# Ordering the experts by their token counts on the chip, with loads addressed from registers and a switch between programs of two and three slot groups

## The chip, the core and the metric

The kernel runs on one core of one Trainium2 chip. The metric is the device time of one execution in microseconds. The engines are TensorE (PE, with PEld for its weight loads), VectorE (DVE), ScalarE (ACT), GpSimd (POOL) and SyncE (SP); SP computes nothing here and issues the weight loads. Each engine has a sequencer that runs its own list of instructions in order.

## What is computed

The reference is a trunk of two layers over 256 tokens of 1024 channels. Each layer mixes tokens (windowed attention beside an mLSTM) and then channels. The channel step of the first layer is a dense SwiGLU; that of the second layer, which the change touches, picks two of eight experts for each token:

```python
def swiglu(x, w13, w2):
    a, g = jnp.split(x @ w13, 2, axis=-1)
    return (jax.nn.silu(a) * g) @ w2

def moe_ffn(x, router_w, router_b, w13, w2):
    logits = (x @ router_w).astype(jnp.float32) + router_b.astype(jnp.float32)
    top_v, top_i = lax.top_k(logits, TOP_K)          # TOP_K = 2 of N_EXPERTS = 8
    wts = jax.nn.softmax(top_v, axis=-1)
    gate = jnp.einsum('bsk,bske->bse', wts, jax.nn.one_hot(top_i, N_EXPERTS, ...))
    y = jnp.zeros_like(x)
    for e in range(N_EXPERTS):
        y = y + gate[..., e:e + 1] * swiglu(x, w13[e], w2[e])
    return y
```

An expert's `w13` is 1024 x 7168 and its `w2` 3584 x 1024, all float32, 44 MB an expert. How many tokens an expert gets is known only when the router has run; the mean is 64.

## The kernel before

Up to the router the kernel runs two mixers and the dense layer; the change leaves that part as it is. `route_tile` picks the experts, writes `posm` (for each token and expert its place among the expert's tokens, or -1), `gate`, and `cnti`, the largest count.

The experts run one after the other (`one_pass`, loop over `e`). Each has 96 slots (`CAP`) in three groups (`NG`) of 32 (`G`). `one_hot` compares `posm` with a ramp, and `gather` multiplies the tokens with it, which gives the expert's tokens transposed (`xe`); this is done for a batch of experts at once (experts 0 and 1, 2 to 4, 5 to 7). The weights are the moving operand of PE and come in pieces of 1 MB, 42 an expert: 28 of `w13` (in four rounds of columns, `ROUNDS`) and 14 of `w2`. For each piece the loop in `batch` issues the products of all three groups; a group has its own 32 columns of the array's weights, and the four quarters of PE's columns work on four column blocks side by side, so that a piece's matmuls go by the number of groups. After a round ACT and DVE apply the SwiGLU; `turn` transposes the hidden rows on PE; `turned_hot` and `scatter` bring the results back to their tokens, and DVE adds them to `x` with the gate. These smaller jobs are put into a list (`todo`) and run behind the second or third piece of a later round.

The pieces are loaded by `Stream`: one list in the order of use, 14 places of 1 MB in the expert stage (`RING`), one DMA each on SP's queue (`pump`, line 89). A piece's load is issued when `done` frees its place, which is when PE has used the piece 14 further up. Which expert a load takes its bytes from is written into the program.

Behind the pass every engine loads `cnti` into a register (line 1034) and jumps twice over a second and third pass (line 1036), which would run for tokens past 96 and 192; with these inputs neither runs (336 loads are 8 x 42). Then the last normalisation and the output follow.

The framework orders the instructions of each engine by a list scheduler; within a pool tile with one buffer the next user waits for the last one.

Of the kernel before, what the change touches and what calls it, by code (L numbers as in the profile page):

```python
# [17 lines left out]
P = 128  # L18
S = 256
# [28 lines left out]
ROUNDS = ((0, 512, (3, 0, 1, 2)), (2048, 512, (0, 1, 2, 3)), (4096, 512, (0, 1, 2, 3)), (6144, 256, (0, 1, 2, 3)))  # L48
RING = ("ring",) * 4 + ("part",) * 6 + ("XL", "XH") + ("more",) * 2


class Stream:
# [3 lines left out]
    def __init__(self, tc, part_pool, part_bufs):  # L56
        self.tc, self.nc, self.behind = tc, tc.nc, None
        self.part_pool, self.part_bufs = part_pool, part_bufs
        self.pieces, self.parts = [], []
        self.raw, self.ready = {}, {}  # L60
        self.places, self.used = {}, {}
        self.loaded = self.split = self.taken = 0
        self.whole_i = -1

# [10 lines left out]
    def pump(self):  # L75

        while self.loaded < len(self.pieces):
# [8 lines left out]
            t = pool.tile([P, n], F32, name="w_raw", tag=tag, bufs=bufs)  # L86
# [43 lines left out]
    def get(self):  # L130
        return self.take(1)[0]

# [10 lines left out]
def hybrid_trunk_kernel(ctx: ExitStack, tc: tile.TileContext, *aps):  # L143
# [71 lines left out]
    def add_experts(s):  # L215


        count = 0

        def to_ring(src):  # L220
            nonlocal count
            s.add(src, (), RING[count % len(RING)])
            count += 1

        for e in range(E):
            w13, w2 = a["exp_w13"][0, e], a["exp_w2"][0, e]
            for c0, w, order in ROUNDS:
                n = 2048 // (4 * w)
                for r0 in range(0, D, n * P):
                    to_ring(w13[r0:r0 + n * P, c0:c0 + 4 * w].rearrange("(k p) f -> p k f", p=P))  # L230

            for r0 in (*range(512, 2048, 256), 0, 256, *range(2048, D_FE, 256)):
                to_ring(rview(w2, r0, 256))

    add_experts(st)
# [17 lines left out]
    rw = const.tile([P, KD, E], F32, name="rw")  # L253
    relb = biasp.tile([NB, HA], F32, name="relb")
# [160 lines left out]
    def router_weights():  # L415
# [4 lines left out]
        nc.vector.memset(ones_b, 1.0)  # L420

# [6 lines left out]
    def route_tile(tt, xt):  # L428
# [24 lines left out]
        if tt:  # L453
            cnt = small.tile([P, 1], F32, name="cnt", tag="cnt")
# [371 lines left out]
    def experts(l, xt):  # L826
# [7 lines left out]
        for t in sides:  # L834
            nc.vector.memset(t[:, NG - 1], 0.0)
# [5 lines left out]
        def aux(shape, name):  # L841
            return pe.tile(shape, F32, name=name, tag="aux", bufs=2)
# [13 lines left out]
        BATCHES = {0: (2, P), 2: (3, CAP), 5: (3, CAP)}  # L856

        def one_pass(s, base):
            pm = posm
            if base:  # L860
                pm = ep.tile([P, 2, E], F32, name="posb")
                nc.vector.tensor_scalar(pm, posm, float(-base), None, op0=ALU.add)
            hot = {}

            def one_hot(e):

                n, w = BATCHES[e]
                t = e2.tile([P, 2, n, w], F32R, name="oneh", tag="oneh")
                for tt in range(2):
                    nc.vector.tensor_tensor(t[:, tt], iota[:, 0:w].unsqueeze(1).to_broadcast([P, n, w]),  # L870
                                            pm[:, tt, e:e + n].unsqueeze(2).to_broadcast([P, n, w]), op=ALU.is_equal)
                hot[e] = t

            def gather(e):

                n, w = BATCHES[e]
                t = e2.tile([P, KD, n, w], F32, name="xe", tag="xe")
                for k in range(KD):
                    pt = aux([P, n, w], "xe")
# [11 lines left out]
            def turned_hot(e):  # L891

                o = e2.tile([P, 2, NG, 4, G], F32, name="hot4", tag="hot4", bufs=1)
# [4 lines left out]
                t = e2.tile([P, NG, S], F32, name="oneT", tag="oneT", bufs=1)  # L898
                for g0, n in ((0, 2), (2, 1)):
                    pt = aux([P, 2, S], "oT")  # L900
# [7 lines left out]
            def scatter(e, i, y, oneT):  # L908

                big, one = side(i).rearrange("p a (t b) -> p a t b", t=2), aux([P, 2, 256], "sc1")  # L910
                for tt in range(2):
                    for g in range(NG):
                        for b in range(4):
# [3 lines left out]
                                             stop=(g == NG - 1), skip_group_check=True)  # L917
                for tt in range(2):
                    for b in range(4):
                        o = big[:, b, tt] if b < NG else one[:, tt]  # L920
                        xt_ = x[:, tt, b * 256:(b + 1) * 256]
                        nc.vector.scalar_tensor_tensor(xt_, o, gate[:, tt, e:e + 1], xt_, op0=ALU.mult, op1=ALU.add)

            def turn(hT, ht, slot, n):

                for g in range(NG):
                    pt = aux([P, n, 4, G], "hT")
# [5 lines left out]
            def turn_one(hT, h4):  # L933

                pt = aux([P, 4, CAP], "hT")
                for i in range(4):
                    nc.tensor.transpose(pt[:, i], h4[:, i * P:(i + 1) * P], ident[0:CAP, 0:CAP])
                nc.vector.tensor_copy(hT[:, 16:20, :], pt)

            with tc.high_priority():  # L940
                one_hot(0)
            xe = gather(0)
            if not base:
                nc.scalar.activation(x, x, AF.Copy, scale=ALPHA)
            todo = []

            def run_todo():
                for f in todo:
                    f()
                todo.clear()  # L950

            def batch(e, n, products, at):

                for k in range(n):
                    i, piece = s.whole()
                    for g in range(NG):
                        products(g, k, piece)
                    s.done(i)
                    if k == at:
                        run_todo()  # L960
            n_side = 0
            for e in range(E):
                if e in BATCHES:
                    cur, first_e = xe, e
                hT = e2.tile([P, D_FE // P, CAP], F32, name="hT", tag="hT", bufs=1)
                hA = e2.tile([P, NG, 512], F32, name="hA", tag="hA", bufs=1)
                hC = e2.tile([P, NG, 256], F32, name="hC", tag="hC", bufs=1)
                s4 = e2.tile([P, NG, 512], F32, name="s4", tag="s4", bufs=1)
                h4 = s4[0:CAP, 0]
                for r, (c0, w, order) in enumerate(ROUNDS):  # L970
                    pt = side(n_side)
                    n_side += 1
                    ks = 2048 // (4 * w)

                    def products(g, n, piece):
                        for j in range(ks):
                            k = n * ks + j
                            for c in range(4):
                                o = order.index(c)
                                mm = nc.tensor.matmul(pt[c * G:(c + 1) * G, g, 0:w],  # L980
                                                      cur[:, k, e - first_e, g * G:(g + 1) * G],
                                                      piece[:, j, o * w:(o + 1) * w], start=(k == 0),
                                                      stop=(k == KD - 1), skip_group_check=True)
                        return mm.ins

                    batch(e, KD // ks, products, 2 if ks == 1 else 1)
                    q = [slice(c * G, (c + 1) * G) for c in range(4)]
                    if r == 0:
                        for g in range(NG):
                            nc.scalar.activation(hA[:, g], pt[:, g], AF.Silu)  # L990
                    elif r == 1:
                        nc.vector.tensor_mul(hA[q[3]], hA[q[3]], pt[q[3]])  # L992
                        nc.scalar.activation(s4[q[3]], pt[q[0]], AF.Silu)  # L993
                        for c in range(4):
                            src = pt[q[1 + c // 2], :, (c % 2) * 256:(c % 2) * 256 + 256]
                            nc.scalar.activation(hC[q[c]], src, AF.Silu)
                    elif r == 2:
                        for g in range(NG):
                            nc.vector.tensor_mul(hA[0:CAP, g], hA[0:CAP, g], pt[0:CAP, g])  # L999
                        for g in range(NG):  # L1000
                            nc.vector.tensor_mul(h4[q[g]], s4[q[3], g], pt[q[3], g])
                        todo.append(lambda hT=hT, hA=hA, h4=h4: (turn(hT, hA, 0, 4), turn_one(hT, h4)))
                    else:
                        nc.vector.tensor_mul(hC, hC, pt[:, :, 0:256])
                        todo.append(lambda hT=hT, hC=hC: turn(hT, hC, 20, 2))
                if e + 1 in BATCHES:
                    one_hot(e + 1)
                    xe = gather(e + 1)
                oneT = turned_hot(e)
                acc = side(n_side)  # L1010
                nf = D_FE // P
                for f0 in range(0, nf, nf // 2):
                    def products(g, n, piece):
                        for j in range(2):
                            f = f0 + 2 * n + j
                            for b in range(4):
                                mm = nc.tensor.matmul(acc[b * G:(b + 1) * G, g, 0:256], hT[:, f, g * G:(g + 1) * G],  # L1017
                                                      piece[:, j, b * 256:(b + 1) * 256], start=(f == 0),
                                                      stop=(f == nf - 1), skip_group_check=True)
                        return mm.ins  # L1020

                    batch(e, nf // 4, products, 2)
                y = e2.tile([P, NG, 256], F32, name="y", tag="y", bufs=1)
                for g in range(NG):
# [4 lines left out]
                todo.append(lambda e=e, i=n_side, y=y, oneT=oneT: scatter(e, i, y, oneT))  # L1029
                n_side += 1  # L1030
            run_todo()

        one_pass(st, 0)
        over = nc.values_load(cnti[0:1, 0:1], min_val=0, max_val=S)
        for base in range(CAP, S, CAP):
            with tc.If(over > base):
# [6 lines left out]
                add_experts(s2)  # L1043
# [66 lines left out]
```

## Time and profile before

| | us |
|---|---|
| median of 3 runs (lowest, highest) | 1582.56 (1582.51, 1584.98) |
| the profiled execution | 1585.02 |
| its span in the profile | 1583.2 |
| mean granted TensorE clock in it | 0.989 |
| PE busy / DVE / ACT | 1544.6 / 508.0 / 378.4 |
| bytes read from HBM | 452.04 MB |

In the profile, PE is the matmuls and PEld the loads of their stationary operand, which run beside them. A float32 matmul is recorded as two. A "q" behind an engine's name is its sequencer. The rows of a window give busy time and count of each engine, then the granted TensorE clock (1.00 is 2.4 GHz, 0.50 is 1.2 GHz), the mean busy share of the 16 DMA engines, and GB/s. The share can pass 1, as it adds the times of packets that overlap.

### The profile page before, as it was taken

The page shows a single profiled execution, that of the slowest core. Times are in us where ns is not written, and L with a number is a line of the kernel's source. Part 1 is how long each engine was busy: PE and PEld are TensorE (multiplying, and loading weights), DVE is VectorE, ACT ScalarE, POOL GpSimd, SP SyncE. Part 2 cuts the span into 40 slices and gives each one's busy share as a digit, 9 for nine tenths or more (in the row PEclk, how much of TensorE's full clock was granted, in tenths as well). Part 3 has the DMA queues.
Part 4 walks back from the last instruction along what each step waited for, and adds up shares of the span by engine and source line. Part 5 has one row for each costly group of instructions (what it writes and reads, how often), then busy time and mean ns, then how long its engine had stood idle before and what let it go on. Part 6 is the DMA issues. An engine that isn't in the chain of part 4 may idle for free. (4 is left out here: it accounts for less than half of the span.)

```text
span 1583.2 us, 35559 instructions
## 1 busy us (share of the span) xinstructions
PE 1544.6 (98%) x16296; PEld 959.3 (61%) x16296; DVE 508.0 (32%) x970; ACT 378.4 (24%) x540; POOL 31.0 (2%) x44
## 2 busy tenths in 40 slices
PE   7999999999999999999999999999999999999994
PEld 6889989998888984354354354354355354354353
DVE  5577775544857763010020010010020010010012
ACT  4555444443445522100110100100110100100100
POOL 2000000000100000000000000000000000000000
PEclk9999999999999997999999999999999999999997
DMA  9634555555533578999979999999979999999950
GB/s 319 194 134 147 179 184 185 186 185 186 181 126 115 166 263 318 390 373 378 392 285 377 390 374 378 390 373 378 391 291 372 390 373 378 399 365 378 387 207 30
DMA packets 112004, 455.55 MB, mean 288 GB/s; under 512 B 7456, under 2 KB 9744, under 8 KB 87264
## 3 DMA queue, kind: packets, MB, share of 16 engines
q1 hardware_dynamic: 108608, 443.05, 74.8%
q0 software_dynamic: 2944, 9.49, 2.1%
q8 instruction: 131, 2.15, 0.5%
q10 hardware_dynamic: 288, 0.59, 0.1%
q14 instruction: 33, 0.27, 0.1%
HBM read 452.04 MB, written 2.63 MB: 287 GB/s over the span
## 5 line engine op out<-in xcount | busy, mean ns | idle before, releaser
L980 PE MATMUL side<-w_raw,xe 128*32 128x512 f32 (+1 forms) x6144 | 592.3, 541 | 0.0
L980 PEld LDWEIGHTS side<-w_raw,xe 128*32 128x32 f32 x6144 | 199.0, 110 | 378.2 <-issue 346.8
L1017 PE MATMUL side<-w_raw,hT 128*32 128x256 f32 x5376 | 302.0, 380 | 0.0
L105 DVE TENSOR_TENSOR w_part<-w_raw,w_part 128x1024 fp32r<-128x1024 f32 x170 | 206.1, 1221 | 141.7 <-ACT w_part L103 141.4
L1017 PEld LDWEIGHTS side<-w_raw,hT 128*32 128x32 f32 x5376 | 173.1, 110 | 116.9 <-issue 6.3
L313 PE MATMUL mm<-xh,w_part 128*128 128x256 f32 x832 | 238.4, 287 | 0.0
L311 PE MATMUL mm<-xh,w_part 128*128 128x256 f32 x832 | 237.7, 286 | 0.0
L312 PE MATMUL mm<-xl,w_part 128*128 128x256 f32 x832 | 237.2, 286 | 0.0
L103 ACT ACTIVATE w_part<-w_raw 128x1024 fp32r<-128x1024 f32 x170 | 179.0, 1058 | 218.3 <-PE mm L313 185.1
L313 PEld LDWEIGHTS mm<-xh,w_part 128*128 128x128 f32 x832 | 159.0, 191 | 4.5 <-issue 4.3
L311 PEld LDWEIGHTS mm<-xh,w_part 128*128 128x128 f32 x832 | 159.1, 191 | 4.2 <-issue 3.8
L312 PEld LDWEIGHTS mm<-xl,w_part 128*128 128x128 f32 x832 | 159.1, 191 | 3.5 <-issue 3.3
L1026 DVE COPY y<-side 128x256 f32<-128x256 f32 x8 | 3.4, 425 | 281.1 <-ACT y L1028 281.1
L992 DVE TENSOR_TENSOR hA<-hA,side 32x1536 f32<-32x1536 f32 x8 | 14.1, 1760 | 247.7 <-issue 247.7
L931 ACT ACTIVATE hT<-hT 128x512 f32<-128x512 f32 (+1 forms) x48 | 21.8, 489 | 238.2 <-PE hT L929 238.2
L999 DVE TENSOR_TENSOR hA<-hA,side 96x512 f32<-96x512 f32 x24 | 15.0, 679 | 150.3 <-PE side L980 150.3
L1028 ACT ACTIVATE y<-side 128x256 f32<-128x256 f32 x16 | 6.1, 383 | 213.2 <-PE side L1017 209.3
L990 ACT ACTIVATE hA<-side 128x512 f32<-128x512 f32 x24 | 12.6, 598 | 169.1 <-PE side L980 169.1
L993 ACT ACTIVATE s<-side 32x1536 f32<-32x1536 f32 x8 | 11.5, 1438 | 166.6 <-DVE hA L992 166.6
L311 PE MATMUL mm<-w_part,xh 128*128 128x512 f32 (+1 forms) x128 | 48.3, 380 | 2.7 <-ACT w_part L103 2.2
L312 PE MATMUL mm<-w_part,xh 128*128 128x512 f32 (+1 forms) x128 | 47.7, 373 | 2.2 <-DVE w_part L105 2.2
L313 PE MATMUL mm<-w_part,xl 128*128 128x512 f32 (+1 forms) x128 | 47.9, 374 | 1.6 <-DVE xl L280 1.6
(275 smaller groups left out, 1272.5 us busy)
## 6 DMA issues: line engine op xcount, KB each, us to landing
w_raw<-in_exp_w_dram SPq DMA_DIRECT2D x336, 1024.0 KB, 6.8
w_raw<-in_ffn_w_dram SPq DMA_DIRECT2D x33, 1024.0 KB, 5.1
w_raw<-in_w_in_dram SPq DMA_DIRECT2D x18, 1024.0 KB, 6.0
w_raw<-in_w_gate_dram SPq DMA_DIRECT2D x16, 1024.0 KB, 5.1
w_raw<-in_w_o_dram SPq DMA_DIRECT2D x8, 1024.0 KB, 4.9
w_raw<-in_w_br_a_dram SPq DMA_DIRECT2D x4, 1024.0 KB, 5.2
w_raw<-in_w_br_m_dram SPq DMA_DIRECT2D x4, 1024.0 KB, 5.1
w_raw<-in_w_in_dram SPq DMA_DIRECT2D x4, 512.0 KB, 8.4
```

The costliest lines, as they stand in the source:

```text
L103: self.nc.scalar.activation(hi, src, AF.Copy)
L105: self.nc.vector.tensor_sub(lo, src, hi.bitcast(F32))
L311: nc.tensor.matmul(ps_ap, lh, rh, start=start, stop=False, **kw)
L312: nc.tensor.matmul(ps_ap, lh, rl, start=False, stop=False, **kw)
L313: nc.tensor.matmul(ps_ap, ll, rh, start=False, stop=stop, **kw)
L931: nc.scalar.activation(dst, pt, AF.Copy)
L980: mm = nc.tensor.matmul(pt[c * G:(c + 1) * G, g, 0:w], cur[:, k, e - first_e, g * G:(g + 1) * G], piece[:, j, o * w:(o + 1) * w], start=(k ...
L990: nc.scalar.activation(hA[:, g], pt[:, g], AF.Silu)
L992: nc.vector.tensor_mul(hA[q[3]], hA[q[3]], pt[q[3]])
L993: nc.scalar.activation(s4[q[3]], pt[q[0]], AF.Silu)
L999: nc.vector.tensor_mul(hA[0:CAP, g], hA[0:CAP, g], pt[0:CAP, g])
L1017: mm = nc.tensor.matmul(acc[b * G:(b + 1) * G, g, 0:256], hT[:, f, g * G:(g + 1) * G], piece[:, j, b * 256:(b + 1) * 256], start=(f == 0), ...
```

## The change

1. `ordering` runs on DVE behind the router. It marks which of experts 1 to 7 have more than 64 tokens and gives the marked ones the places 2, 4, 6, 1, 3, 5, 7 in this order, the others what is left. It writes the expert of each place and the number of the program to `metai`, and copies `posm` and `gate` in the order of the places (`pmP`, `gtP`). Expert 0 stays first. Three small constants are added (`ordc`).
2. SP loads the seven experts from `metai` into registers, and the loads of places 1 to 7 take their address from them.
3. All engines load the number of the program and, behind expert 0, go through one `tc.Switch` with three arms. Arm 0, 1 and 2 hold places 1 to 7 with the first 3, 5 or 7 of the list 2, 4, 6, 1, 3, 5, 7 at three groups and the rest at two. With two groups every loop over groups is shorter: products, SwiGLU, transposes, scatter.
4. The batches of the gather are place 0 (with expert 1's slots beside it, unused), 1 to 3, 4 and 5, 6 and 7: four where there were three.
5. Tiles of the expert stage that came from pools are made once and reused in turn, so that all arms have the same addresses; the memsets of the third bank of `side` go.

```diff
+PLACES = (2, 4, 6, 1, 3, 5, 7)
+ARMS = (3, 5, 7)
...
+            def src():
+                if ordered and e:
+                    i = s.which[e - 1]
+                    return take(w[0, bass.ds(i, 1)].rearrange("a r f -> (a r) f"))
+                return take(w[0, e])
...
-        for t in sides:
-            nc.vector.memset(t[:, NG - 1], 0.0)
...
+        def ordering():
...
+            nc.vector.memset(meta, 0.0)
+            nc.vector.tensor_scalar(big, cnt8[:, 1:E], float(CAP - G), None, op0=ALU.is_gt)
+            nc.vector.tensor_tensor(t49, tri7, across(big), op=ALU.mult)
+            nc.vector.tensor_reduce(pre, t49, X, ALU.add)
+            nc.vector.tensor_reduce(m[:, 0:1], big, X, ALU.add)
...
+            nc.vector.tensor_tensor(sl, place_of.unsqueeze(2).to_broadcast([P, n1, n1]), across(rank), op=ALU.is_equal)
+            for src, dst in ((j7, meta[:, 0:n1]), (posm[:, 0, 1:E], pmP[:, 0, 1:E]), (posm[:, 1, 1:E], pmP[:, 1, 1:E]),
+                             (gate[:, 0, 1:E], gtP[:, 0, 1:E]), (gate[:, 1, 1:E], gtP[:, 1, 1:E])):
+                nc.vector.tensor_tensor(t49, sl, across(src), op=ALU.mult)
+                nc.vector.tensor_reduce(dst, t49, X, ALU.add)
+            nc.vector.tensor_scalar(meta[:, 0:n1], meta[:, 0:n1], 1.0, None, op0=ALU.add)
+            for i, limit in enumerate(ARMS[:-1]):
+                nc.vector.tensor_scalar(meta[:, 9 + i:10 + i], m[:, 0:1], float(limit), None, op0=ALU.is_gt)
...
-                BATCHES = {0: (2, P), 2: (3, CAP), 5: (3, CAP)}
+                BATCHES = {0: (1, P), 1: (3, CAP), 4: (2, P), 6: (2, P)}
...
-                    for g in range(NG):
-                        products(g, k, piece)
-                    s.done(i)
+                        for g in range(ng):
+                            products(g, k, piece)
+                        s.done(i)
...
+            ordering()
+            which.extend(nc.values_load(metai[0:1, i:i + 1], engines=[mybir.EngineType.SP], min_val=1, max_val=E - 1)
+                         for i in range(n1))
+            arm_i = nc.values_load(metai[0:1, 8:9], min_val=0, max_val=len(ARMS) - 1)
+            expert(s, 0, NG, c)
+            for arm in tc.Switch(arm_i, len(ARMS)):
+                sa, ca = s.fork(), dict(c, todo=list(c["todo"]))
+                for e in range(1, E):
+                    expert(sa, e, NG if PLACES.index(e) < ARMS[arm] else NG - 1, ca)
```

On PE, at the passage from expert 0 to the next one, before (a product of a `w2` piece is `side<-w_raw,hT`, one of a `w13` piece `side<-w_raw,xe`, the scatter `<-y,oneT`):

```order
L1017 MATMUL side_5838<-w_raw,hT 32x256 x248
L980 MATMUL side_5839<-w_raw,xe 32x512 x36
L916 MATMUL side_5838<-y,oneT 128x256 x3
L916 MATMUL sc_6849<-y,oneT 128x256
L916 MATMUL side_5838<-y,oneT 128x256 x3
```

And the same place now, in the first arm:

```order
L1111 MATMUL side_5842<-w_raw,hT 32x256 x232
L1136 TENSOR_LOAD metai
L1222 SWITCH_STRIDE
L1222 ISA x2
L1138 BRANCH_PREFETCH_HINT
L1074 MATMUL side_5843<-w_raw,xe_5846 32x512 x24
L1018 MATMUL side_5842<-y,oneT 128x256 x3
```

The switch stands between the last product of expert 0 and the first of the next place, and three pieces are 24 matmuls there where they were 36.

On SP, where the loads of the first 14 expert pieces end, before:

```order
L89 DMA w_raw<-in_exp_w_dram 128x2048 x14
L1034 TENSOR_LOAD cnti
L1034 ISA x2
L89 DMA w_raw<-in_exp_w_dram 128x2048 x10
L89 DMA w_raw<-in_exp_w_dram 128x2x1024 x18
L89 DMA w_raw<-in_exp_w_dram 128x2048 x24
```

And now, to the switch, with six of the eight loads of `metai` and 12 of the 14 loads of place 1 left out between the two fences:

```order
L102 DMA w_raw<-in_exp_w_dram 128x2048 x14
L1146 TENSOR_LOAD cnti
L1146 ISA x2
L1134 TENSOR_LOAD metai
L1134 ISA x2
```

```order
L1136 TENSOR_LOAD metai
L1136 ISA x2
L102 DMA w_raw<-in_exp_w_dram 128x2048 x10
L102 DMA w_raw<-in_exp_w_dram 128x2x1024 x18
L102 ISA
L102 DMA w_raw<-in_exp_w_dram 128x2048
```

```order
L102 DMA w_raw<-in_exp_w_dram 128x2048
L1222 SWITCH_STRIDE
L1222 ISA x2
L1138 BRANCH_PREFETCH_HINT
L102 ISA
```

Behind the 14 loads stand eight register loads more, each load of places 1 to 7 has one instruction in front of it, and SP comes to the switch when 56 loads (42 of expert 0, 14 of place 1) are issued.

On DVE, at the end of the pass, before:

```order
L1026 COPY y<-side_5839 128x256
L922 SCALAR_TENSOR_TENSOR x<-side_5839,gate,x 128x256 x6
L922 SCALAR_TENSOR_TENSOR x<-sc_13284,gate,x 128x256 x2
L1034 TENSOR_LOAD cnti
L1036 COMPARE_AND_BRANCH
```

And now, at the end of the first arm:

```order
L1118 COPY y<-side_5843 128x256
L1024 SCALAR_TENSOR_TENSOR x<-side_5843,gtP,x 128x256 x6
L1024 SCALAR_TENSOR_TENSOR x<-aux_5844,gtP,x 128x256 x2
L1222 UNCONDITIONAL_BRANCH
L1138 BRANCH_PREFETCH_HINT
```

The jump behind the additions leads over the other two arms, to the load of `cnti` and the two branches that stood there before.

## Rows read from the trace of the kernel before

**Rows 1.** The page, parts 1 and 5: engine busy; group | busy us, mean ns | idle before.

```profile
PE 1544.6 (98%) x16296; PEld 959.3 (61%) x16296; DVE 508.0 (32%) x970; ACT 378.4 (24%) x540; POOL 31.0 (2%) x44
...
L980 PE MATMUL side<-w_raw,xe 128*32 128x512 f32 (+1 forms) x6144 | 592.3, 541 | 0.0
...
L1017 PE MATMUL side<-w_raw,hT 128*32 128x256 f32 x5376 | 302.0, 380 | 0.0
```

**Rows 2.** Waits of SP's queue, 640 to 1583 us: total us, times, longest.

```profile
SPq L89 <- PE side L980: 502.5, 214, 5.1
SPq L89 <- PE side L1017: 235.0, 93, 5.9
```

**Rows 3.** Timeline of PE in three stretches: start us, length us, line, tiles, count.

```profile
607.23 5.40 PE L980 MATMUL side<-w_raw,xe 128*32 128x512 f32 x28
...
726.72 7.91 PE L980 MATMUL side<-w_raw,xe 128*32 128x512 f32 x72
...
1532.09 26.97 PE L1017 MATMUL side<-w_raw,hT 128*32 128x256 f32 x496
```

**Rows 4.** Windows of one expert each: length, PE, PEld, DVE, ACT, POOL, clock, share, GB/s.

```profile
971.00:1087.40 116.40, 116.40 (x1520) 51.59 (x1516) 12.09 (x24) 10.58 (x18) 0.00 (x0) 1.00 0.99 383
1087.40:1212.40 125.00, 125.00 (x1552) 56.35 (x1548) 13.91 (x28) 12.33 (x22) 0.00 (x0) 1.00 0.92 352
```

**Rows 5.** Timeline of SP's queue, 721 to 735 us.

```profile
721.78 13.23 SPq L89 DMA_DIRECT2D w_raw<-in_exp_w_dram  x6
```

**Rows 6.** The page, part 6: DMA issues, KB each, median us to landing.

```profile
w_raw<-in_exp_w_dram SPq DMA_DIRECT2D x336, 1024.0 KB, 6.8
```

**Rows 7.** Windows of 40 us in the expert stage.

```profile
800.00:840.00 40.00, 40.00 (x571) 23.21 (x573) 4.54 (x12) 4.26 (x10) 0.00 (x0) 1.00 0.78 285
1360.00:1400.00 40.00, 40.00 (x433) 14.57 (x422) 5.71 (x7) 6.12 (x8) 0.00 (x0) 1.00 1.02 394
```

**Rows 8.** Windows at the highest shares of the DMA engines.

```profile
645.00:650.00 5.00, 5.00 (x52) 1.56 (x48) 0.00 (x0) 0.00 (x0) 0.00 (x0) 1.00 1.04 359
...
600.00:605.00 5.00, 2.82 (x12) 2.10 (x12) 4.57 (x28) 0.55 (x3) 0.00 (x0) 0.50 1.03 428
655.00:685.00 30.00, 30.00 (x336) 11.95 (x328) 5.49 (x8) 6.32 (x8) 0.00 (x0) 1.00 1.02 409
```

**Rows 9.** Timeline of DVE: first of 17 small operations of the router, and the memset behind.

```profile
600.29 0.16 DVE L436 TENSOR_TENSOR route<-lg,rb 128x8 f32<-128x8 f32 x1
...
602.65 0.48 DVE L835 MEMSET side<- 128x512 f32 x1
```

**Rows 10.** Line 1034, the register loads: duration ns min/median/max, first and last start.

```profile
L1034 SPq TENSOR_LOAD <-cnti x1: 461/461/461, 602.6 to 602.6; - x1
...
L1034 SPq FUSED_REGOPS  x1: 182/182/182, 603.1 to 603.1; - x1
...
L1034 PEldq TENSOR_LOAD <-cnti x1: 491/491/491, 1561.9 to 1561.9; - x1
```

**Rows 11.** Line 1036, the two jumps over the second passes, same columns.

```profile
L1036 PEldq COMPARE_BRANCH  x2: 3418/4152/4886, 1562.5 to 1566.1; - x2
L1036 DVEq COMPARE_BRANCH  x2: 56/64/72, 1564.2 to 1567.2; - x2
...
L1036 DVEq EVENT_SEMAPHORE  x2: 21/21/21, 1567.1 to 1571.7; - x2
```

**Rows 12.** Line 89, the loads.

```profile
DMA to landing us min/median/max: 4.7/6.5/13.6
```

**Rows 13.** Timeline of DVE behind the jumps: in brackets idle before and what ended it.

```profile
1571.85 1.29 DVE L298 BATCH_NORM_STATS2 bs<-x 128x6 f32<-128x512 f32 x2 [5.21 <-DVEq L1036]
```

**Rows 14.** Windows with PE partly idle, and the clock behind the second.

```profile
202.40:207.40 5.00, 3.18 (x18) 2.16 (x17) 5.00 (x9) 3.23 (x4) 0.81 (x1) 1.00 0.00 0
588.30:593.30 5.00, 3.06 (x24) 2.73 (x24) 4.93 (x12) 2.14 (x3) 1.20 (x2) 1.00 0.94 328
595.00:600.00 5.00, 4.70 (x24) 4.34 (x23) 4.90 (x19) 4.97 (x6) 0.00 (x0) 0.50 1.00 415
```

More of the change, by code (lines that the diff above doesn't have):

```diff
@@ L1 @@
+import copy
 import math
@@ L131, in get, with fork @@
         return self.take(1)[0]
+    def fork(self):
+        s = copy.copy(self)
+        s.raw, s.used, s.loads = dict(self.raw), dict(self.used), dict(self.loads)
+        return s
 def cols_views(n, w):
@@ L906, in turned_hot, with scatter @@
                 return t
-            def scatter(e, i, y, oneT):
-                big, one = side(i).rearrange("p a (t b) -> p a t b", t=2), aux([P, 2, 256], "sc1")
+            def scatter(e, i, y, oneT, ng):
+                big, one = side(i).rearrange("p a (t b) -> p a t b", t=2), aux([P, 2, 256])
                 for tt in range(2):
-                    for g in range(NG):
+                    for g in range(ng):
                         for b in range(4):
@@ L961, in one_pass @@
-            n_side = 0
-            for e in range(E):
-                if e in BATCHES:
[L964 to L969, printed above, removed]
+                    nc.tensor.transpose(pt[:, i], h4[0:ng * G, i * P:(i + 1) * P],
+                                        ident[0:ng * G, 0:ng * G])
@@ new lines, in turn_one, with expert, run_todo, batch @@
+                nc.vector.tensor_copy(hT[:, 16:20, 0:ng * G], pt)
+            def expert(s, e, ng, c):
+                if e in BATCHES:
+                    c["cur"], c["first"] = c["xe"], e
+                cur, j0 = c["cur"], e - c["first"]
+                def run_todo():
+                    for f in c["todo"]:
+                        f()
+                    c["todo"] = []
+                def batch(n, products, at):
+                    for k in range(n):
+                        i, piece = s.whole()
+                        for g in range(ng):
+                            products(g, k, piece)
+                        s.done(i)
+                        if k == at:
+                            run_todo()
@@ L977, in products @@
                             k = n * ks + j
[L978 to L983, printed above, removed]
@@ L984, in products @@
-                        return mm.ins
-                    batch(e, KD // ks, products, 2 if ks == 1 else 1)
-                    q = [slice(c * G, (c + 1) * G) for c in range(4)]
+                            for q in range(4):
+                                o = order.index(q)
+                                nc.tensor.matmul(pt[q * G:(q + 1) * G, g, 0:w], cur[:, k, j0, g * G:(g + 1) * G],
+                                                 piece[:, j, o * w:(o + 1) * w], start=(k == 0), stop=(k == KD - 1),
+                                                 skip_group_check=True)
@@ L1011, in one_pass @@
-                nf = D_FE // P
[L1012 to L1022, printed above, removed]
@@ L1023, in one_pass, with down @@
-                y = e2.tile([P, NG, 256], F32, name="y", tag="y", bufs=1)
-                for g in range(NG):
+                    c["xe"] = gather(e + 1)
+                turned_hot(e, ng)
+                i_side = c["side"]
+                c["side"] += 1
+                acc = side(i_side)
+                nf = D_FE // P
+                def down(g, n, piece):
+                    for j in range(2):
+                        f = 2 * n + j
+                        for b in range(4):
+                            nc.tensor.matmul(acc[b * G:(b + 1) * G, g, 0:256], hT[:, f, g * G:(g + 1) * G],
+                                             piece[:, j, b * 256:(b + 1) * 256], start=(f == 0), stop=(f == nf - 1),
+                                             skip_group_check=True)
@@ L1025, in one_pass @@
+                batch(nf // 2, down, 2)
+                for g in range(ng):
                     if g == 1:
@@ L1028, in one_pass @@
                         nc.scalar.activation(y[:, g], acc[:, g, 0:256], AF.Copy)
-                todo.append(lambda e=e, i=n_side, y=y, oneT=oneT: scatter(e, i, y, oneT))
-                n_side += 1
-            run_todo()
+                c["todo"].append(lambda: scatter(e, i_side, y, oneT, ng))
+                if e == E - 1:
+                    run_todo()
+            with tc.high_priority():
+                one_hot(0)
+            c = {"xe": gather(0), "todo": [], "side": 0}
+            if base:
+                for e in range(E):
+                    expert(s, e, NG, c)
+                return
+            nc.scalar.activation(x, x, AF.Copy, scale=ALPHA)
+            ordering()
[7 more added lines that the diff above has]
+                    expert(sa, e, NG if PLACES.index(e) < ARMS[arm] else NG - 1, ca)
+        which = []
+        st.which = which
         one_pass(st, 0)
@@ L1068, in _constants @@
     c[:, 640:768] = p[None, :]
+    j = np.arange(E - 1)
+    c[:, 1152:1201] = (j[None, :] < j[:, None]).reshape(1, -1)
+    c[:, 1201:1208] = j[None, :]
+    c[:, 1208:1215] = [PLACES.index(i) for i in range(1, E)]
     dist = 255 - np.arange(NREL)
```

172 lines of the change are left out of this document (109 added, 63 removed).

## The prediction

> **What bounds the kernel now.** The page comes first: TensorE (PE) is busy 98% of the span, and the matmuls on expert weights, lines 980 and 1017, are its largest groups, with no idle time in front of them [rows 1]. Next the waits of SP, whose queue issues every weight load: in the expert stage it waits for PE, 307 times and 737 us in all [rows 2]. So this stage, from the first product at 607.23 us to the last at 1532.09 + 26.97 = 1559.06 us [rows 3], runs at PE's pace, and the loads follow. The reader is then to see how little room lies behind PE. An expert takes 116.4 us, or 125.0 us when the gather of a batch falls in it [rows 4]. SP issues six loads in 13.23 us [rows 5], so a piece takes (13.23 - 0.33)/5 = 2.58 us, and a piece is 1024 KB [rows 6]: 406 GB/s. At this demand the DMA engines' busy share is already 1.00 and more [rows 7, 8]. The change makes PE quicker; what the DMA engines can then give decides.
>
> **What the change removes on PE.** The reference's routing, worked out on its inputs, gives expert 0 70 tokens and experts 1 to 7 57, 64, 71, 49, 66, 82 and 53. Three of these seven exceed 64, so the switch takes the first program: expert 0 and places 2, 4, 6 with three groups, places 1, 3, 5, 7 with two. A piece of a two-group place has two thirds of the matmuls: 1.72 us. Of the 116.4 us, 42 x 2.58 = 108.4 are products; the other 8.0 (scatter, turning the hidden rows) go by groups too, so a two-group place needs 72.2 + 5.4 = 77.6 us. Four of them free 4 x 38.8 = 155 us of PE.
>
> **What it adds on PE.** (a) Four gathers where there were three: that of three experts costs 125.0 - 116.4 = 8.6 us [rows 4], one of two experts 8.6 x 256/288 = 7.6 us. The first of them moves into expert 0; two gathers of two experts come later. (b) The ordering on VectorE (DVE): some 20 of its small operations now stand between the copies that free the buffers of the first gather. Rows of such operations come 0.14 us apart (17 in 2.36 us [rows 9]), so 2.8 us, less the two memsets of 0.48 us that go: 2 us, with bounds of 0 (hidden beside PE) and 5. (c) The switch: each engine loads the arm's number (0.49 us on PE [rows 10]) and jumps. PE's two jumps in this trace took 3.42 and 4.89 us [rows 11]; I take 5 us for load and jump together, between 0.5 (the jump was prefetched) and 8. SP reaches it with the loads of 14 pieces issued; before that it loads eight more registers, 0.46 + 0.18 us each [rows 10], while expert 0 is PE-bound. Both are hidden by the full ring, until SP were 14 x 2.58 = 36 us late. A register in the address makes an issue longer than 0.33 us by an amount that no row shows; it is hidden while an issue stays under a piece's 2.5 us.
>
> So expert 0 ends at 726.72 (the next one's first product [rows 3]) + 8.6 + 2 = 737.3, the first arm starts at 742.3, and its first piece is used up at 744.0.
>
> **What is late next: the loads.** With 14 places, piece 56 of the 336 can be issued at 744.1. From there PE uses up a two-group piece in 1.72 us, faster than any rate that this trace shows for loads, and the ring runs empty within that place. A three-group place takes 116.4/42 = 2.77 us a piece and wins back only a few pieces, which the next two-group place eats. The loads then run without a pause to the end: the last lands at 744.1 + 4.7 (shortest landing [rows 12]) + 279 c, with c the time of one piece on a queue that is never empty.
>
> No row shows c over such a length. The best 5 us, when places had just come free at once, moved 428 GB/s: c = 2.45 us. The other bound is the rate over the busy share of a long window, 394/1.02 = 386 GB/s: c = 2.72 us [rows 7, 8]. Between them lies the longest stretch with the share over 1.00 throughout: 409 GB/s for 30 us, c = 2.564 us [rows 8]. I take that one. Then 279 c = 715.3 us, and PE ends the last piece at 744.1 + 4.7 + 715.3 + 1.7 = 1465.8.
>
> A rule speaks against this. The Trainium skill, page "DMA: Bandwidth & Descriptors", section "Where 436 GB/s comes from", says that transfers between HBM and SBUF are bound on the HBM side, at about 358 GB/s for a core. By it c would be 2.93 us and the time 1593 us. The trace disagrees so far: 409 GB/s for 30 us and 394 for 40 us lie above it [rows 7, 8]; no run here has a queue that stays full for 700 us.
>
> **The tail.** From the last product to the end are 1583.2 - 1559.06 = 24.1 us. With two groups the last place has one copy and 8 of 24 scatter matmuls less, some 1.3 us. But the arm ends with one more taken jump ahead of the two that skip the second passes. On DVE, which sets the end, the next operation starts 5.21 us late for its sequencer [rows 13], whose two jumps, begun at 1564.2 and 1567.2, end 2.9 and 4.5 us later [rows 11]; one more costs 3.7 us, between 0 (fetched under the last additions) and 5. Tail: 24.1 - 1.3 + 3.7 = 26.5 us.
>
> Sum: span 1465.8 + 26.5 = 1492.3 us. The profiled run took 1585.02 us, 1.8 over its span, and is 2.5 over the median of 1582.56. So 1492.3 + 1.8 - 2.5 = 1491.6, say 1492 us, 5.7% faster. Of the 155 us freed on PE, 91 arrive.
>
> **Rivals.**
> A. A full queue gives no more than the long windows: c = 2.72, time 1491.6 + 279 x 0.156 = 1535 us. For it: no 40-us window passes 394 GB/s. Against it: SP waited for PE in those, and pauses are in them (285 GB/s at a share of 0.78 where a gather falls [rows 7]).
> B. PE stays the bound: 742.3 + 3 x 116.4 + 4 x 77.6 + 2 x 7.6 + 26.5 = 1444, time 1443 us. It needs c under 2.39 us, 439 GB/s; no row reaches that.
> C. The other side: the rate falls when the queue stays full, since PE's pace had spaced the loads. From c = 2.564 + 91/279 = 2.89 us, 363 GB/s, the gain is gone. For it: with loads piling up behind expert 0's start, 5 us at a share of 1.04 moved 359 GB/s [rows 8]; held to the end that is c = 2.92 and 1591 us. Against it: the 30 us right behind it gave 409.
> D. PE's clock. In a two-group place PE would work 77.6 of 107.7 us, 72%, in bursts. If the granted clock fell from 1.00 (2.4 GHz) to 0.50 there, such a place would take 155 us and the whole 1753 us; the gain is gone once it takes 112 us. For it: after 3.06 busy us of 5, on 8-column matmuls, the clock stood at 0.50. Against it: with 3.18 of 5 it stayed at 1.00 [rows 14]. The Trainium skill, page "TensorE: Matmul & The Clock Gate", section "HAM oscillation — how this bites in real kernels", warns of such a loop, little work and then a wait for a load, in which every tile starts at half clock. No row here shows it for waits of 0.8 us.
> E. It does not do what it says: the arm with seven three-group places is taken. Then PE has its old work, 6.6 us more of gathers (8.6 + 2 x 7.6 - 2 x 8.6), 2 + 5 + 3.7 us: 1600 us. Against it: the counts.
>
> **How the numbers follow.** The forecast (c of 2.45 to 2.64) has a chance of 0.62, A (2.64 to 2.80) 0.24, B 0.03, a rate between A and no gain 0.04, C 0.03, D 0.02, E 0.02. The forecast's own range is 1460 to 1513; with A, and the few us of jumps and ordering, the range is 1462 to 1535. A difference under 0.2% can't be told from none here. Faster by more: forecast, A, B and nearly all between A and no gain, 0.93. The same: 0.01. Slower: C, D and E with the rest, 0.06.
>
> **What would show it.** In the new profile SP's waits for PE should all but go outside expert 0 and turn into waits of PE for loads, some 50 us in all, nearly all in two-group places. The DMA share should hold at 1.0 with about 409 GB/s from some 820 us to the end of the loads, which should land some 30 us after their issue (median 6.8 now), as up to 13 are queued; the last about 2 us ahead of the last product. The matmuls of the two groups should fall by a sixth. It would be wrong if PE waits for nothing (B), if the rate is under 390 GB/s while SP doesn't wait (A, C), or if the granted clock drops in a two-group place (D).

## The result and the profile after

The changed kernel takes 1488.51 us (median of 4 runs, 1488.1 to 1490.78) against 1582.53 us before (1582.0 to 1584.98): a ratio of 0.9406, 95% interval 0.939 to 0.9422. The forecast was 1492 us. The profiled execution took 1488.1 us, its span is 1486.2 us.

The page of the changed kernel, parts 1 and 5, as in [rows 1]:

```profile
PE 1406.6 (95%) x14312; PEld 886.5 (60%) x14312; DVE 502.9 (34%) x989; ACT 366.1 (25%) x524; POOL 31.6 (2%) x45
...
L1074 PE MATMUL side<-w_raw,xe 128*32 128x512 f32 (+1 forms) x5120 | 501.7, 542 | 22.1 <-DMA w_raw<-in_exp_w_dram 19.8
...
L1111 PE MATMUL side<-w_raw,hT 128*32 128x256 f32 x4480 | 258.0, 380 | 17.5 <-DMA w_raw<-in_exp_w_dram 16.4
```

Both groups of products have a sixth fewer matmuls (6144 to 5120, 5376 to 4480), each as long as before. In front of them there is idle time now, nearly all of it ended by a load. PE's waits between the first product of place 1 and the last product of all (total us, times, longest):

```profile
PE side L1074 <- DMA w_raw<-in_exp_w_dram: 19.8, 35, 0.7
PE side L1111 <- DMA w_raw<-in_exp_w_dram: 16.4, 28, 1.4
PE side L1074 <- issue: 2.3, 1, 2.3
PE side L1111 <- SPq L1148: 1.1, 2, 0.6
...
```

These are 36.2 us in 63 waits for loads, and 2.3 us once, at the switch. The two waits behind L1148 are those of the last two pieces; they too end as the pieces land. The timeline of PE at the three stretches of [rows 3]: the first product, the first one behind the switch, the last piece.

```profile
604.78 4.51 PE L1074 MATMUL side<-w_raw,xe 128*32 128x512 f32 x22
...
736.44 5.36 PE L1074 MATMUL side<-w_raw,xe 128*32 128x512 f32 x48 [2.28 <-issue]
...
1460.28 1.93 PE L1111 MATMUL side<-w_raw,hT 128*32 128x256 f32 x32 [0.57 <-SPq L1148]
```

So the switch leaves PE idle for 2.28 us. The last product ends at 1462.2, 24.0 us ahead of the end (24.1 before). The next two views show where the places differ and what stays the same. Windows of places 1 to 4 (columns as in [rows 4]), and one window over nearly the whole arm:

```profile
736.44:818.44 82.00, 79.39 (x1028) 34.99 (x1028) 11.42 (x30) 7.17 (x13) 0.00 (x0) 1.00 1.01 403
818.44:934.40 115.96, 115.95 (x1501) 50.58 (x1504) 12.09 (x24) 9.82 (x16) 0.00 (x0) 1.00 1.02 415
934.40:1033.25 98.85, 87.92 (x1065) 37.29 (x1057) 11.28 (x25) 9.47 (x19) 0.00 (x0) 1.00 1.02 414
1033.25:1149.61 116.36, 116.36 (x1500) 50.93 (x1504) 12.07 (x24) 9.81 (x16) 0.00 (x0) 1.00 1.02 415
```

```profile
760.00:1460.00 700.00, 662.44 (x8408) 285.83 (x8400) 72.83 (x145) 62.14 (x111) 0.00 (x0) 1.00 1.01 410
```

A three-group place takes 116 us, as before, and PE has no gap in it. A two-group place takes 82 us while the full ring of expert 0 lasts, and 97 to 99 us after that. One of each (places 3 and 4) is 215 us, 84 pieces at 2.56 us. The loads are the constant: 410 GB/s for 700 us, which is 2.557 us for a piece of 1.049 MB, at a granted clock of 1.00 throughout.

SP's side came out otherwise than forecast. Its waits over the stretch of [rows 2], and the time of a load from issue to landing (page, part 6, as in [rows 6]):

```profile
SPq L102 <- DMA w_raw<-in_exp_w_dram: 298.0, 164, 2.9
SPq L102 <- PE side L1074: 159.9, 104, 5.1
SPq L102 <- PE side L1111: 110.6, 64, 5.8
```

```profile
w_raw<-in_exp_w_dram SPq DMA_DIRECT2D x336, 1024.0 KB, 19.7
```

Of SP's waits for PE, 737 us in [rows 2], 270 us are left (159.9 + 110.6), and 298 us of waits for loads are new: each load waits on its semaphore for the load eight before it, as the program has eight semaphores that its loads take in turn, and then for its place. Counted from issues and landings, seven others are on their way whenever one lands, in every place from the second on; before it was mostly one to three. 19.7 us is 7.7 pieces of 2.557 us.

### The profile page after: what moved, and what is told of

Same layout as the page of the kernel before. It is cut to its first block, busy times and chain, and to the rows that moved or that the text cites. A ratio compares the mean times of both kernels' runs of the same rounds, so it can differ in the third digit from the quotient of the medians.

```text
span 1486.2 us, 32301 instructions
## 1 busy us (share of the span) xinstructions
PE 1406.6 (95%) x14312; PEld 886.5 (60%) x14312; DVE 502.9 (34%) x989; ACT 366.1 (25%) x524; POOL 31.6 (2%) x45
## 5 line engine op out<-in xcount | busy, mean ns | idle before, releaser
L1074 PE MATMUL side<-w_raw,xe 128*32 128x512 f32 (+1 forms) x5120 | 501.7, 542 | 22.1 <-DMA w_raw<-in_exp_w_dram 19.8
L1074 PEld LDWEIGHTS side<-w_raw,xe 128*32 128x32 f32 x5120 | 161.7, 110 | 345.4 <-issue 276.8
L1111 PE MATMUL side<-w_raw,hT 128*32 128x256 f32 x4480 | 258.0, 380 | 17.5 <-DMA w_raw<-in_exp_w_dram 16.4
L1111 PEld LDWEIGHTS side<-w_raw,hT 128*32 128x32 f32 x4480 | 141.4, 110 | 122.6 <-DMA w_raw<-in_exp_w_dram 25.6
L1084 DVE TENSOR_TENSOR hA<-hA,side 32x1536 f32<-32x1536 f32 (+1 forms) x8 | 11.9, 1494 | 207.5 <-issue 170.8
L1033 ACT ACTIVATE hT<-aux 128x512 f32<-128x512 f32 (+1 forms) x40 | 18.2, 488 | 207.2 <-PE aux L1031 207.2
L1085 ACT ACTIVATE s<-side 32x1536 f32<-32x1536 f32 (+1 forms) x8 | 9.8, 1224 | 141.2 <-DVE hA L1084 141.2
## 6 DMA issues: line engine op xcount, KB each, us to landing
w_raw<-in_exp_w_dram SPq DMA_DIRECT2D x336, 1024.0 KB, 19.7
```

The source lines that it names most:

```text
L1033: nc.scalar.activation(dst, pt, AF.Copy)
L1074: nc.tensor.matmul(pt[q * G:(q + 1) * G, g, 0:w], cur[:, k, j0, g * G:(g + 1) * G], piece[:, j, o * w:(o + 1) * w], start=(k == 0), stop=( ...
L1084: nc.vector.tensor_mul(hA[q[3], 0:ng], hA[q[3], 0:ng], pt[q[3], 0:ng])
L1085: nc.scalar.activation(s4[q[3], 0:ng], pt[q[0], 0:ng], AF.Silu)
```

## The experiments

In six of the eight kernels one part was changed against the first, in which a branch replaces the switch; the last goes on from the seventh. The kernel before, beside which they ran, took 1583.28 us (the first four) and 1583.83 us (the others); differences of that size, half a microsecond, say nothing between the two groups. All of them but the last build only the first of the three programs, which is the one that these counts take.

**1. A branch in place of the switch.**

```diff
-            for arm in tc.Switch(arm_i, len(ARMS)):
+            arm = 0
+            with tc.If(arm_i < 1):
```

> A compare and a branch on the arm's number stand in place of the switch, and only the first of the three programs is built (it is the one that these counts take). Theory (the loads are the bound, and all that delays PE ahead of the 57th piece counts in full): PE's 2.28 us at the switch go, since the program now follows without a jump, and so does the jump at its end: 2.3 us, and 0 to 4 more in the tail, 1484 us (1481 to 1487). Rival (all of it is hidden behind the loads): 1488 us, no change. Rival (the switch costs far more than PE's idle time shows): under 1478 us.

Measured: 1484.02 us (1483.16 to 1485.35), ratio 0.9374 (0.9361 to 0.9386). Timeline of PE at the first product of place 1, and of DVE behind its last addition:

```profile
733.73 1.47 PE L1074 MATMUL side<-w_raw,xe 128*32 128x512 f32 x12
```

```profile
1470.35 2.47 DVE L327 BATCH_NORM_STATS2 bs<-x 128x6 f32<-128x512 f32 x4 [4.54 <-DVEq L1149]
```

The 2.28 us in front of place 1 are gone. Place 1 starts 2.71 us earlier than in the changed kernel (736.44), and the last piece, first fence of experiment 6, comes earlier by the same 2.71 us (1457.57 for 1460.28). DVE's wait behind the jumps is 4.54 us where the changed kernel has 6.30 (last timeline of this section), so all of the 4.5 us are seen. What delays PE ahead of place 1 isn't hidden by the loads; it moves them all.

**2. Two groups in all seven places.** This leaves out the slots 64 to 95 of three experts.

```diff
-                    expert(sa, e, NG if PLACES.index(e) < ARMS[arm] else NG - 1, ca)
+                    expert(sa, e, NG - 1, ca)
```

> As the one with the branch, and all seven places run two slot groups (the slots 64 to 95 of three experts are left out). Theory (the loads are the bound from the first place on, 2.56 us a piece): their stream neither starts earlier nor runs faster, so the time is that of the one with the branch within 3 us, about 1484 us, and PE's waits for loads grow by the 3 x 38.8 = 116 us of work that went. Rival (PE and its waits set the pace, each place by its own work): three places fall from 116 to some 98 us, 54 us less, 1430 us; with no bound by the loads at all 1368 us.

Measured: 1483.74 us (1481.99 to 1484.51). PE's waits from 720 to 1470 us, and a window from place 2 on:

```profile
PE side L1074 <- DMA w_raw<-in_exp_w_dram: 64.5, 114, 1.2
PE side L1111 <- DMA w_raw<-in_exp_w_dram: 46.2, 67, 1.7
```

```profile
760.00:1455.00 695.00, 575.92 (x6872) 220.88 (x6864) 65.50 (x135) 52.61 (x96) 0.00 (x0) 1.00 1.01 411
```

PE has 116 us less to do and the time does not move. Its waits for loads grow from 36 us in 61 gaps (experiment 1) to 111 us in 181, and its waits for other engines by 7 us. That this is 82 and not 116 us more I put down to the modelled ends of matmuls, which would have to cover some 0.3 us of each gap; this is an estimate that no view shows (with it, the 36 us are 54, and experiments 1 and 3 differ by 54). The rate is 411 GB/s, the same as with three three-group places. So the rate is no property of how PE takes the pieces, and the rival by which each place has its own time has fallen.

**3. Half the bytes.**

```diff
-            self.nc.sync.dma_start(t, src)
+            if i >= self.first_whole + 56:
+                h = (slice(0, P), slice(0, 1), slice(0, b // (3 - a)))
+                self.nc.sync.dma_start(t[h], src[h])
+            else:
+                self.nc.sync.dma_start(t, src)
```

> As the one with the branch, and from the 57th piece on each load brings only half of its 1024 KB; the products read what the place held before in the other half. PE's work, the ordering, the gathers and the ring stay. Theory: with the loads out of the way PE is the bound again and waits for nothing: 734.2 + 3 x 116.4 + 4 x 77.6 + 2 x 7.6 = 1409 at the last product, 22 to 24 of tail, 1.9 around it: 1433 us (1428 to 1440), with two-group places of 77.6 us. Rival 1 (a two-group place takes 97 to 99 us by itself, through its shorter runs of products): 1484 us. Rival 2 (each load has a fixed price, whatever its bytes): 1484 us at half the GB/s.

Measured: 1430.21 us (1428.16 to 1431.46). Windows of places 3 (two groups and a gather, without its first product), 4 (three groups) and 7 (two groups), and PE's only wait in the arm:

```profile
926.69:1010.15 83.46, 83.46 (x1064) 38.67 (x1059) 11.25 (x24) 9.11 (x18) 0.00 (x0) 1.00 0.78 259
1010.57:1126.13 115.56, 115.56 (x1502) 50.69 (x1498) 12.09 (x24) 10.22 (x17) 0.00 (x0) 1.00 0.67 196
1325.57:1403.73 78.16, 78.16 (x1031) 34.94 (x1024) 8.65 (x16) 7.58 (x14) 0.00 (x0) 1.00 0.60 198
```

```profile
PE aux L1022 <- ACT y L1124: 0.6, 1, 0.6
```

Without the loads' bound a two-group place takes 78.2 us (77.6 forecast), 5.3 to 5.7 more with a gather (7.6 forecast). As the number of loads is the same, it is not a price for each load that bounds the kernel. The packets of a load fall too, from 204 to 145 in the mean, so this run alone doesn't tell bytes from packets. The landings of experiment 1 do: pieces whose rows are 4 KB have twice the packets of those with 8 KB rows, and land 2.60 us apart where the others land 2.52 us apart. It is the bytes.

**4. Three groups in all places.**

```diff
-ARMS = (3, 5, 7)
+ARMS = (7, 7, 7)
```

> As the one with the branch, but the program has three groups in all places; the ordering, the register addresses and the four gathers stay. Theory: PE is the bound, 734.2 + 7 x 116.4 + 2 x 7.6 = 1564 at the last product, 24 of tail, 1.9 around it: 1590 us, 8 us over the kernel before, the price of the machinery without the switch (6.6 more of gathers, some 1.3 for the ordering). Rival (the machinery costs far more and eats the missing 61 us of the 155 freed on PE): 1625 us or more.

Measured: 1590.17 us (1589.35 to 1591.01), ratio 1.0044 (1.0029 to 1.006). The ordering, the addresses from registers and the gathers cost 6.9 us (8 forecast) on a PE-bound kernel, and nothing like 61. PE waits for no load (0.6 us for one small copy in the whole stage). Experiments 3 and 4 together measure what two groups free on PE: 1590.17 - 1430.21 = 160 us (155 forecast; the shorter tail and the cheaper gathers of experiment 3 are in the 160); of this 54 us go back to the loads (1484.02 - 1430.21).

**5. The three-group places first.**

```diff
-PLACES = (2, 4, 6, 1, 3, 5, 7)
+PLACES = (1, 2, 3, 4, 5, 6, 7)
```

> As the one with the branch (1484.0 us), but the three three-group experts stand at places 1, 2, 3 in place of 2, 4, 6; the work is the same. Theory: while three-group places follow each other PE is the bound and the ring stays full, so the loads stand still for part of the time; the two-group places behind are bound by the loads. Place 4 starts at 733.7 + 3 x 116.4 + 7.7 = 1090.6, the 183rd piece is issued 1.9 later and lands 7.5 after that, the other 153 take 2.56 us each, to 1491.7: 34 us more than with the branch alone (1457.5), 1518 us (1511 to 1524). Rival (each place has its own time, 116 or 99 us, whatever stands ahead): 1484 us.

Measured: 1518.64 us (1517.81 to 1519.3), ratio 0.9585 (0.957 to 0.9599). Windows of places 1 to 3, and of places 5 to 7 with two groups:

```profile
735.12:1092.12 357.00, 357.00 (x4584) 159.03 (x4580) 40.19 (x84) 33.38 (x58) 0.00 (x0) 1.00 0.97 371
...
1175.55:1494.60 319.05, 262.29 (x3062) 98.10 (x3066) 28.98 (x59) 22.99 (x42) 0.00 (x0) 1.00 1.00 408
```

The same work in another order costs 34.6 us. For 357 us PE has no gap and the loads move 371 GB/s, and what they don't move then is missing when PE could be fast. With the places alternating, the ring carries a three-group place's lag of some 116 - 107.5 = 9 us over to the next place, and the loads don't pause.

**6. Ten places in the ring.**

```diff
-RING = ("ring",) * 4 + ("part",) * 6 + ("XL", "XH") + ("more",) * 2
+RING = ("ring",) * 4 + ("part",) * 6
```

> As the one with the branch (1484.0 us), with 10 places in the ring in place of 14. Theory: from the first two-group place on the loads never pause, so what counts is how many pieces are still to be loaded when PE uses up the first piece of place 1: four places fewer leave four more pieces at 2.56 us, 1494 us (1491 to 1499; more if PE's lag in a three-group place, 3 to 6 pieces, now stops the loads). Rival (never more than 8 loads are on their way, so places beyond those 8 give nothing): 1484 us.

Measured: 1497.09 us (1496.06 to 1497.3), ratio 0.9449 (0.9434 to 0.9463). The last piece with 14 places (experiment 1) and with 10, and DVE behind its last addition with 10:

```profile
1457.57 1.93 PE L1111 MATMUL side<-w_raw,hT 128*32 128x256 f32 x32 [0.57 <-SPq L1149]
```

```profile
1468.25 1.93 PE L1108 MATMUL side<-w_raw,hT 128*32 128x256 f32 x32 [0.56 <-SPq L1146]
...
1483.54 2.47 DVE L327 BATCH_NORM_STATS2 bs<-x 128x6 f32<-128x512 f32 x4 [7.05 <-DVEq L1146]
```

The last piece comes 10.7 us later, 2.7 us for each place (2.56 forecast). The other 2.4 us are a longer wait behind the same two jumps, which the theory doesn't have. A jump runs from its COMPARE_BRANCH to the EVENT_SEMAPHORE behind it, as in [rows 11]; first and last start in experiment 1 (L1149) and with ten places (L1146):

```profile
L1149 DVEq COMPARE_BRANCH  x2: 56/62/69, 1463.3 to 1466.4; - x2
L1149 DVEq EVENT_SEMAPHORE  x2: 21/21/21, 1466.3 to 1470.2; - x2
```

```profile
L1146 DVEq COMPARE_BRANCH  x2: 63/66/69, 1474.0 to 1479.9; - x2
...
L1146 DVEq EVENT_SEMAPHORE  x2: 21/21/21, 1477.0 to 1483.4; - x2
```

The jumps are no longer here (3.0 and 3.5 us, against 3.0 and 3.8), but the second begins 2.9 us after the first has ended, where it was 0.1 us. What fills that stretch stays open.

The run also answers a rival of the whole account: that not the rate of the loads binds, but the limit of eight on their way. With ten places the ring often holds the next load back, and when a load lands only five to seven others are on their way; the rate stays the same.

```profile
820.00:1450.00 630.00, 601.20 (x7476) 257.24 (x7465) 67.00 (x134) 56.48 (x101) 0.00 (x0) 1.00 1.02 414
```

Experiment 1 has 413 GB/s in the same window. That only eight loads are on their way doesn't make the other places useless: they hold pieces that have landed, and it is these that PE spends when it turns fast.

**7. Gathers only in two-group places.** The part of the ordering that copies `posm` in the order of the places now runs ahead of the first gather, so that this can take expert 0 and place 1 together.

```diff
-                BATCHES = {0: (1, P), 1: (3, CAP), 4: (2, P), 6: (2, P)}
+                BATCHES = {0: (2, P), 2: (2, P), 4: (2, P), 6: (2, P)}
...
             with tc.high_priority():
+                if not base:
+                    ordering(True)
                 one_hot(0)
```

> As the one with the branch (1484.0 us), but the ordering comes ahead of the first gather, which so takes expert 0 and place 1 together; the gathers of places 2 and 3, 4 and 5, 6 and 7 follow in places 1, 3 and 5, all of two groups. Expert 0 loses its second gather. Theory: PE ahead of the 57th piece loses 8.6 us of gather and waits 2 to 3.5 us more for the ordering, and the gathers in two-group places take the place of waits for loads: 5 to 6.5 us less, 1478 us (1476 to 1481). Rival (the head start is hidden, the loads have slack elsewhere): 1484 us. Rival (the ordering ahead of the first gather, some 15 operations one behind the other, takes as much as the gather did): 1484 us or more.

Measured: 1479.09 us (1477.7 to 1479.74), ratio 0.9334 (0.9321 to 0.9347). Expert 0 with the two gathers of experiment 1, then here; and PE's wait ahead of the first gather here:

```profile
605.59:733.72 128.13, 128.13 (x1521) 57.02 (x1524) 12.84 (x30) 13.99 (x24) 0.00 (x0) 0.99 0.89 338
```

```profile
610.94:730.01 119.07, 119.07 (x1489) 52.17 (x1492) 8.50 (x12) 12.26 (x20) 0.00 (x0) 0.99 0.93 356
```

```profile
PE aux L990 <- DVE oneh L976: 4.3, 1, 4.3
```

Expert 0 loses 9.1 us, the ordering takes 4.3 us back (2 to 3.5 forecast), and the gathers cost nothing where PE would wait anyway.

**8. One jump at the end.** All three programs are built again; what these counts don't take lies under one branch.

```diff
+        with tc.If(flags[2] > 0):
+            for n in (1, 2):
+                with tc.If(flags[n - 1] > 0):
+                    arms[0](n)
             for base in range(CAP, S, CAP):
                 with tc.If(over > base):
```

> As the one with the pairs, with all three programs built, and the other two programs and the second passes put under one common branch, so that the normal way has one jump at its end and not two. Theory: VectorE, which sets the end, sat idle for 4.54 us behind its last addition for two jumps of some 3 to 3.9 us; with one the wait falls to 0.5 to 1.3 us: 3.3 to 4 us less than with the pairs, 1474.5 us (1472 to 1477). Rival (the jump is hidden and the wait is for something else): 1478 us.

Measured: 1474.47 us (1473.25 to 1475.53), ratio 0.9307 (0.9294 to 0.932), the fastest here: 14 us under the changed kernel. DVE behind its last addition, in this kernel and in the changed one:

```profile
1462.10 2.47 DVE L327 BATCH_NORM_STATS2 bs<-x 128x6 f32<-128x512 f32 x4 [1.65 <-DVEq L1168]
```

```profile
1474.82 2.47 DVE L327 BATCH_NORM_STATS2 bs<-x 128x6 f32<-128x512 f32 x4 [6.30 <-DVEq L1148]
```

One jump less is 3.0 us of DVE's wait (4.61 with the pairs, 1.65 here) and 4.6 us of time. Most of the other 1.6 us lies ahead of the jump: in the profiled runs the last product ends 1.4 us earlier here (1454.14 for 1455.56 us), and the first gather began 2.7 us earlier (604.95 for 607.62), behind a part of the kernel that is the same in both. So the wait in [rows 13] is the jumps, one behind the other. The Trainium skill, page "Runtime: NRT & Kernel Launch", section "Instruction fetch mechanics", says that a taken branch out of the loaded code must wait for a fetch. Jumps of 3 to 5 us agree, and so do the DMA packets between the last product and DVE's next operation, with the pairs and here; all of them are of the kind `instruction`:

```profile
DMA packets 11, 0.11 MB, mean 11 GB/s; under 512 B 0, under 2 KB 0, under 8 KB 0
```

```profile
DMA packets 4, 0.04 MB, mean 5 GB/s; under 512 B 0, under 2 KB 0, under 8 KB 0
```

That DVE waits for just these packets, and not another engine, is not shown.

## Why the prediction was right, and where it wasn't

- **The freed work.** 155 us were forecast; experiments 3 and 4 give 160. Right.
- **The loads take over.** Right in kind, and shown by experiments 2 and 3.
- **The pace of the loads.** c was taken as 2.564 us from 30 us of [rows 8], and the arm shows 2.557 over 700 us. That they agree so well is luck. In those 30 us the loads did not set the pace: SP waited for PE most of the time (last line of this point: total us, times, longest, 655 to 685 us), issued a load every 2.57 us, and had two or three others on the way. So that row measured PE's pace of 2.58 us a piece, the first paragraph's own number, and said of the loads only that they can follow it. A's long windows were held to PE's pace in the same way. It so happens that the loads' own pace, which experiment 2 shows with PE idle for a sixth of the time, is under 1% faster. The busy share of the DMA engines doesn't tell the two apart: 1.02 stands beside 394 GB/s in [rows 7] and beside 414 in the arm.

```profile
SPq L89 <- PE side L980: 21.3, 10, 2.1
```

- **PE's waits.** Some 50 us forecast, 36.2 shown as idle, with modelled ends beside them; 54 us by the times of experiments 1 and 3. All lie in two-group places, as forecast.
- **The start of the loads' stretch.** 744.1 us was forecast for the issue of piece 56; SP's queue has it at 738.41. The switch cost 2.28 us of PE and not 5. Expert 0 took 604.78 to 734.16, 129.4 us for the 130.1 forecast (119.5 + 8.6 + 2). It began 2.5 us earlier than in the trace before, which no term of the forecast has.
- **The first landing** took 7.7 us and not 4.7, as two other loads were still ahead of it; this took back 3 of the 5.7 us.
- **The tail.** 26.5 us forecast, 24.0 measured. The jump at the end of the arm was priced at 3.7 us, with a lower bound of nothing if it falls under the last additions, and that is what happened: it begins at 1465.4 us and the jumps behind it begin at 1466.4, while the additions run to 1468.5. The 1.1 us by which DVE's wait passes that of [rows 13] come from those two, 4.1 us each.

```profile
L1148 DVEq COMPARE_BRANCH  x2: 63/70/77, 1466.4 to 1470.6; - x2
...
L1148 DVEq EVENT_SEMAPHORE  x2: 21/21/21, 1470.5 to 1474.7; - x2
```

- **The sum.** The span came out 6.1 us under the forecast (1486.2 for 1492.3), and the median 3.1 us (1488.51 for 1491.6): the profiled run was taken for 2.5 us over the median, as in the kernel before, and here it is 0.4 under. So the 3 us are what is left of several small errors that partly cancel.
- **What failed: the signs on SP's side.** "SP's waits for PE should all but go outside expert 0" was wrong in its logic: SP runs ahead whenever the ring is full of loads that are not used yet, and it then waits for a place; 190 us of such waits are left between 736 and 1462 us. And "some 30 us after their issue, as up to 13 are queued" was wrong by the limit of eight: 19.7 us. Neither entered the sum, because the rate holds with eight on their way, and by experiment 6 with fewer.
- **Rivals.** B needs 439 GB/s; experiment 2 offers PE's time in plenty and gets 411. C: a queue that stays full didn't lower the rate. The rule of the Trainium skill, page "DMA: Bandwidth & Descriptors", section "Where 436 GB/s comes from", weighed in the prediction, would have given 1593 us; 410 GB/s for 700 us on this core lies above its 358. D: the clock stood at 1.00 in every place, and in experiment 2 with PE busy 576 of 695 us. E: the counts took the first arm, as the two-group places show.

## What to carry to other kernels

When two resources are close, here 116 us of PE against 107.5 us of loads for an expert, making one faster buys only the distance to the other: work out the other's pace from a stretch in which nothing holds it up, and start counting at the point from which it never pauses. A rate read while the first resource sets the pace is only a bound, however busy the second looks; where the trace has no longer stretch of the right kind, as here, a run in which the first resource has less to do (experiment 2) gives it. From there on every microsecond ahead of that point counts in full, a buffer more is worth one transfer, and added work is free where the faster engine waits. Alternate the slow and the fast pieces, so that the buffer evens them out.

## What the hardware showed that was not expected

- One core drew 410 GB/s from HBM for 700 us, with pieces of 1 MB and eight loads on their way; with six to eight the rate was the same, and half the bytes took the bound away entirely.
- Rows of 4 KB in place of 8 KB cost a 1 MB load 0.08 us of 2.5 (experiment 1).
- With 181 waits of up to 1.7 us for the 294 pieces of seven places (experiment 2) the granted clock stayed at 1.00.
- The two jumps behind the pass kept DVE waiting 4.54, 4.61, 5.21, 6.30 and 7.05 us in five programs that differ elsewhere.
- A gather of two experts costs 5.3 to 5.7 us in a two-group place with the loads out of the way, and 124.12 - 116.44 = 7.7 us in a three-group place of experiment 4.
